# Gate and up of a transformer block's last row block from seven half products instead of eight

## The chip, the cores and the metric

The kernel runs on one core of a Trainium2 chip: TensorE (matmuls, with its own path for loading weights), VectorE, ScalarE, POOL (GpSimd) for elementwise work, and SP, whose queue issues nearly all transfers between the memories. The metric is device time in microseconds of one execution, compared by the median of several.

## The reference

One layer over x of 2048 x 1024 (float32), with D_FF = 2816:

```
a = rms_norm(h, ln_mix_pre);  proj = a @ w_in           # split among four mixers
mix = concat[S5, HGRN2, FoX, mLSTM] @ w_out             # all causal in time
h = h + rms_norm(mix, ln_mix_post)
a = rms_norm(h, ln_ffn_pre)
ff = (silu(a @ w_ffn_gate) * (a @ w_ffn_up)) @ w_ffn_down
h = h + rms_norm(ff, ln_ffn_post)
```

What concerns us here is `a @ w_ffn_gate` and `a @ w_ffn_up`, both 2048 x 1024 by 1024 x 2816.

## The kernel before

The 2048 rows are handled in four blocks of 512 (`BLK`), called first, second, third and last block here (b = 0 to 3). After the input projection of all rows, each block goes through `Attn.proj(b)` (the output projection with its norms), the mixers of the next block (`mixers(b + 1)`: mLSTM, the FoX attention and others), and the feed-forward `ffn(b)`, whose body is `run`. The mixers are written ahead of the feed-forward, so that its matmuls fill what the mixers leave of TensorE.

The order of instructions on each engine is not written out. The framework plans the program ahead of time with a simulated timeline: an instruction takes its place on its engine's queue when its inputs and its buffer are ready in that timeline, earlier lines of the program first. On the chip each queue then runs in that fixed order, and a queue whose head waits holds everything behind it.

Matmuls are made of float32 operands in two parts, high and low (a rounded value and the rest), as three matmuls: high x high, low weight x high, high weight x low. `split_load` brings weights: in the first block it loads the raw tile, ScalarE makes the high part (L87), POOL the low part (L88), and both are stored to DRAM (L92). The later blocks load the stored parts (L83). Weight tiles for gate and up lie in a ring `w_ring` of four places (tiles `wh`, `wl`), raw tiles in a ring `w_raw` of two (`wr`), tiles of x in a ring of two (`xtile`), and the weights of down in four places (`dh`, `dl`).

`Attn.proj(b)` makes, for each of four groups t of 128 rows, the second half of the output projection (L1385), the first norm and residual with a row tile `b_xt` of x (loaded at L1418, used at L1419), the second norm (L1424), and eight 128 x 128 transposes (L102) whose results are split into `b_ah` and `b_al` (ScalarE L104, VectorE L105).

In `run`, `gate_up` takes a column tile f of 128 columns of D_FF: 24 matmuls for gate and 24 for up (8 slices of the 1024 inputs, three parts), each 128 x 128 weights by 512 rows (L1468). The first pair, f = 0 and 1, is done in two halves of 256 rows each, so that it can start when t = 0 and 1 are there. Then come the gate's activation on ScalarE and VectorE (L1472 to L1478). `down` takes two tiles f at a time: 48 matmuls (L1493) in eight parts, each added into `b_acc` on VectorE (L1498). There are 22 tiles f, that is eleven pairs. The FoX attention adds its probabilities up on POOL (L900) and splits them on VectorE (L896).

## Time and profile before

| | |
|---|---|
| median of 3 runs | 2812.64 us (2810.97 to 2820.45) |
| profiled execution | 2810.77 us, its span 2809.1 us |
| TensorE busy | 2692.9 us, 96% |
| VectorE, ScalarE, POOL busy | 55%, 28%, 30% |
| DMA | 605.04 MB, mean 215 GB/s |

The span runs from the first to the last instruction of the profiled execution. A matmul's busy time includes its way through the array, in which the next one has already started; the rate at which TensorE works is the distance between two starts. "Releaser" is what ended an engine's wait.

### The profile page before, as it was taken

How to read it: one execution, taken by the hardware profiler on the slowest of the kernel's cores; microseconds unless marked ns; L12 is line 12 of the kernel's file. 1: busy time of each engine (PE TensorE's matmuls, PEld its weight loads, DVE VectorE, ACT ScalarE, POOL GpSimd, SP SyncE). 2: the span in 40 equal slices, each digit the busy share in tenths (PEclk: the TensorE clock that was granted, in tenths of full speed). 3: DMA queues.
4: the chain of work that ended last, by engine and by line, in shares of the span. 5: the costliest groups of instructions: out<-in, count | busy, mean ns of one | idle time of the engine just before them, and what ended most of it. 6: DMA issues, size and time to landing. Idle time of an engine off the chain costs nothing.

```text
span 2809.1 us, 39028 instructions
## 1 busy us (share of the span) xinstructions
PE 2692.9 (96%) x14294; PEld 2271.5 (81%) x14294; DVE 1550.5 (55%) x2522; ACT 779.0 (28%) x1502; POOL 841.8 (30%) x927
## 2 busy tenths in 40 slices
PE   6798989999999999899899999999999999999998
PEld 5787987988888778788787778888878788888886
DVE  7958456575325665876366656645666654322333
ACT  5322326322323343324221232223122331200001
POOL 7653311242216567542211234202022430100001
PEclk9999999999999999999999999999999999999999
DMA  6573695544779987686756566575656557755553
GB/s 229 201 258 114 184 300 181 169 163 161 259 205 299 317 268 267 212 306 231 273 169 215 191 199 210 174 280 195 210 181 195 193 175 246 279 198 187 194 193 136
DMA packets 323103, 605.04 MB, mean 215 GB/s; under 512 B 56160, under 2 KB 146144, under 8 KB 322656
## 3 DMA queue, kind: packets, MB, share of 16 engines
q1 hardware_dynamic: 321888, 602.48, 63.8%
q8 instruction: 113, 1.85, 0.3%
q14 instruction: 78, 0.64, 0.1%
q0 software_dynamic: 1024, 0.07, 0.0%
HBM read 428.42 MB, written 173.35 MB: 214 GB/s over the span
## 4 chain that ended last, share of the span: by engine, by line
PE 76%; DVE 8%; DMA 7%; issue 2%; SPq 2%; ACT 2%; POOL 2%; POOLq 0%; DVEq 0%; ACTq 0%
PE pf L1468 31%; PE pf L1493 15%; PE pf L288 7%; PE pf L1385 5%; PE pf L270 5%; PE ps L903 2%; DVE hQ L511 1%; PE ps L828 1%; PE ps L887 1%; PE ps L886 1%; DVE hA L525 1%; PE ps L521 1%; PE pt L102 1%; DMA b_xt<-in_x_dram 1%; DVE mcv L353 1%
## 5 line engine op out<-in xcount | busy, mean ns | idle before, releaser
L1468 PE MATMUL pf<-b_ah,wh 128*128 128x512 f32 (+1 forms) x1536 | 579.3, 378 | 4.5 <-ACT b_ah L104 4.3
L1468 PE MATMUL pf<-b_ah,wl 128*128 128x512 f32 (+1 forms) x1536 | 579.1, 378 | 0.0
L1468 PE MATMUL pf<-b_al,wh 128*128 128x512 f32 (+1 forms) x1536 | 577.5, 378 | 0.0
L1493 PE MATMUL pf<-dh,g_h 128*128 128x512 f32 x1408 | 456.8, 395 | 2.2 <-DVE b_acc L1498 1.9
L1468 PEld LDWEIGHTS pf<-b_ah,wh 128*128 128x128 f32 x1536 | 290.0, 189 | 60.4 <-ACT b_ah L104 5.3
L1468 PEld LDWEIGHTS pf<-b_ah,wl 128*128 128x128 f32 x1536 | 289.8, 189 | 54.2
L1468 PEld LDWEIGHTS pf<-b_al,wh 128*128 128x128 f32 x1536 | 288.7, 189 | 53.9
L1493 PEld LDWEIGHTS pf<-dh,g_h 128*128 128x128 f32 x1408 | 263.8, 188 | 58.8 <-DVE b_acc L1498 3.6
L1493 PE MATMUL pf<-dl,g_h 128*128 128x512 f32 x704 | 276.7, 393 | 0.0
L1498 DVE TENSOR_TENSOR b_acc<-b_acc,pf 128x512 f32<-128x512 f32 x320 | 216.3, 684 | 102.0 <-PE pf L1493 99.7
L900 POOL TENSOR_TENSOR f_accs<-f_accs,f_pe 128x512 f32<-128x512 f32 (+3 forms) x144 | 172.8, 1200 | 280.0 <-ACT f_pe L894 274.8
L88 POOL TENSOR_TENSOR wl<-wr,wh 128x1024 fp32r<-128x1024 f32 (+2 forms) x76 | 186.6, 2459 | 191.2 <-ACT wh L87 128.5
L896 DVE TENSOR_TENSOR f_pl<-f_pe,f_ph 128x512 fp32r<-128x512 f32 (+3 forms) x160 | 179.4, 1128 | 97.6 <-ACT f_ph L895 82.0
L288 PE MATMUL pf<-wl,aTh 128*128 128x256 f32 (+2 forms) x768 | 221.0, 288 | 0.0
L288 PE MATMUL pf<-wh,aTl 128*128 128x256 f32 (+2 forms) x768 | 220.4, 287 | 0.0
L288 PE MATMUL pf<-wh,aTh 128*128 128x256 f32 (+2 forms) x768 | 220.2, 287 | 0.0
L1473 DVE SCALAR_TENSOR_TENSOR g_th<-g_th,pf 128x512 f32<-128x512 f32 x88 | 60.3, 685 | 192.9 <-ACT g_th L1472 192.6
L1472 ACT ACTIVATE g_th<-pf 128x512 f32<-128x512 f32 x88 | 52.6, 598 | 403.3 <-PE pf L1468 403.2
L270 PE MATMUL pf<-aTh,wh 128*128 128x512 f32 (+1 forms) x400 | 160.3, 401 | 3.2 <-ACT aTh L104 3.2
L270 PE MATMUL pf<-aTh,wl 128*128 128x512 f32 (+1 forms) x400 | 157.9, 395 | 0.0
L1474 DVE TENSOR_TENSOR g_th<-g_th,pf 128x512 f32<-128x512 f32 x88 | 60.3, 685 | 176.1 <-PE pf L1468 175.7
L270 PE MATMUL pf<-aTl,wh 128*128 128x512 f32 (+1 forms) x400 | 156.8, 394 | 0.5 <-DVE aTl L105 0.5
(511 smaller groups left out, 4841.1 us busy)
## 6 DMA issues: line engine op xcount, KB each, us to landing
dh<-wd_0h SPq DMA_DIRECT2D x66, 256.0 KB
dl<-wd_0l SPq DMA_DIRECT2D x66, 256.0 KB
dh<-wd_1h SPq DMA_DIRECT2D x66, 256.0 KB
dl<-wd_1l SPq DMA_DIRECT2D x66, 256.0 KB
wr<-in_w_ffn_gate_dram SPq DMA_DIRECT2D x22, 512.0 KB
wr<-in_w_ffn_up_dram SPq DMA_DIRECT2D x22, 512.0 KB
dr<-in_w_ffn_down_dram SPq DMA_DIRECT2D x44, 256.0 KB
f_KB<-kb_d SPq DMA_DIRECT2D x80, 132.0 KB
```

The lines of the kernel that those rows point to most:

```text
L88: nc.gpsimd.tensor_tensor(lo, r, f32(hi), ALU.subtract)
L270: nc.tensor.matmul(l3(pt)[:, cut], lhsT=x[k][:, s], rhs=a[:, cut, k], start=(n == 0), stop=(n == 23))
L288: nc.tensor.matmul(pt[:, :w], lhsT=a[:, t, k], rhs=x[k], start=(n == 0), stop=(n == 23))
L896: nc.vector.tensor_tensor(pl[:, cs], pe[:, cs], f32(ph[:, cs]), ALU.subtract)
L900: nc.gpsimd.tensor_tensor(accs[:, cs], accs[:, cs], pe[:, cs], ALU.add)
L903: nc.tensor.matmul(o, lhsT=w, rhs=r[:, cs], start=(kt + n == 0), stop=(kt + n == NK))
L1385: nc.tensor.matmul(pt, lhsT=a[:, t, k], rhs=w, start=(first and i == 0), stop=(last and i == 2))
L1468: nc.tensor.matmul(l3(pt)[:, s], lhsT=x[:, k], rhs=a[:, s, k], start=(k == 0 and i == 0), stop=(k == KD - 1 and i == 2))
L1473: nc.vector.scalar_tensor_tensor(th, th, 1.0, pts[0], ALU.add, ALU.mult)
L1474: nc.vector.tensor_tensor(th, th, pts[1], ALU.mult)
L1493: nc.tensor.matmul(pt, lhsT=a[:, s], rhs=w[:, 0], start=(m == 0), stop=(m == 3 * len(fs) - 1))
L1498: nc.vector.tensor_tensor(acc[:, t, ns], acc[:, t, ns], pt, ALU.add)
```

## The change

In the last block alone, gate and up of a pair of column tiles are formed from seven products of halves. The rows (t = 0, 1 against t = 2, 3), the 1024 inputs (first and second 512) and the pair (f even, f odd) are halved, and the seven products, numbered 0 to 6 in the code, are those of a Strassen-like scheme (Winograd's form): sums of row halves (`T1` to `T4`) times sums of weight halves. A product is 24 matmuls of 128 x 128 weights by 256 rows, gate and up side by side in one PSUM tile; VectorE and ScalarE put the products together in a tile `C`, and `gated` does the activation from there.

Products 0, 2 and 5 use stored parts of plain weight halves. The other four use sums of weights: `Halves.make` forms them in the second block for gate and in the third for up, one step per pair: two raw tiles loaded, four POOL operations, four stores to DRAM. In the last block `Halves.load` brings such a sum into the ring's low tile, and ScalarE and POOL split it there. `Halves.put` takes the place of the eight transposes in `proj`: the same eight for t = 0 and 1 (products 0 and 2), twenty each for t = 2 and 3. There the x tile lies in `w_raw` and not in the x ring. The transposed operands lie in a tile `U`, which takes the place of the mixers' buffers.

```diff
@@ -96,7 +96,7 @@
 def transpose_parts(c, pool, tag, x, dh, dl):
     nc = c.nc
-    for h in range(0, KD, 4):
+    for h in range(0, x.shape[1] // P, 4):
         pt = pool.tile([P, 512], F32, name="pt", tag=tag)
         for j in range(4):
             nc.tensor.transpose(pt[:, j * P:(j + 1) * P], x[:, (h + j) * P:(h + j + 1) * P], c.ident)
@@ -1331,6 +1331,71 @@
     c.nc.scalar.activation(junk[:, 0:n], x, AF.Square, accum_out=out)
+class Halves:
+    def __init__(self, c):
+        self.c = c
+        self.w = [x[0].rearrange("(k p) n -> p k n", p=P) for x in (c.w_ffn_gate, c.w_ffn_up)]
+        self.pairs = c.w_ffn_gate.shape[2] // (2 * P)
+        self.sums = {(q, i): c.dram.tile([P, D], F32, name=f"ws{q}_{i}") for q in range(self.pairs) for i in (1, 3, 4, 6)}
+    def make(self, pool, q, m):
+        nc = self.c.nc
+        rs = [pool.tile([P, D], F32, name=n, tag=n) for n in ("ws_1", "ws_2")]
+        for i, r in enumerate(rs):
+            f = 2 * q + i
+            nc.sync.dma_start(r.rearrange("p (k n) -> p k n", k=KD), self.w[m][:, :, f * P:(f + 1) * P])
+        (X11, X12), (X21, X22) = ((r[:, 0:512], r[:, 512:]) for r in rs)
+        for i, s, x, y, op in ((3, X11, X11, X21, ALU.subtract), (4, X21, X21, X22, ALU.add),
+                               (1, X22, X22, X11, ALU.subtract), (6, X12, X12, X22, ALU.subtract)):
+            nc.gpsimd.tensor_tensor(s, x, y, op)
+            nc.sync.dma_start(self.sums[q, i][:, m * 512:m * 512 + 512], s)
+    def load(self, q, i):
+        c, nc = self.c, self.c.nc
+        hi, lo = (c.pw.tile([P, WRING], F32R, name=n, tag=n)[:, 0:D] for n in ("wh", "wl"))
+        if (q, i) in self.sums:
+            nc.sync.dma_start(f32(lo), self.sums[q, i])
+            nc.scalar.activation(hi, f32(lo), AF.Copy)
+            nc.gpsimd.tensor_tensor(lo, f32(lo), f32(hi), ALU.subtract)
+        else:
+            k0, f = {0: (0, 0), 2: (512, 0), 5: (512, 1)}[i]
+            for t, part in ((hi, 0), (lo, 1)):
+                for m, n in enumerate("gu"):
+                    nc.sync.dma_start(f32(t[:, m * 512:m * 512 + 512]),
+                                      c.parts[f"w{n}{2 * q + f}"][part][:, k0:k0 + 512])
+        return hi, lo
+    def operand(self, i, t):
+        u = self.U[:, 2 * i + t].rearrange("p (d k t) -> p d k t", d=2, k=4)
+        return u[:, 0], u[:, 1]
+    def put(self, t, xs, rows):
+        c, nc = self.c, self.c.nc
+        a, b = slice(0, 512), slice(512, D)
+        if t < 2:
+            new = ((0, xs[t][:, a]), (2, xs[t][:, b]))
+        else:
+            x, x1 = xs[t - 2], xs[t]
+            s1, s2 = rows(), rows()
+            T1, T2, T3, T4 = s1[:, a], s1[:, b], s2[:, a], s2[:, b]
+            nc.vector.tensor_tensor(T1, x1[:, a], x[:, a], ALU.subtract)
+            nc.vector.tensor_tensor(T2, x1[:, b], T1, ALU.subtract)
+            nc.gpsimd.tensor_tensor(T3, x1[:, b], x1[:, a], ALU.subtract)
+            nc.vector.tensor_tensor(T4, x[:, b], T2, ALU.subtract)
+            new = ((1, T2), (3, T3), (4, T1), (5, T4), (6, x1[:, b]))
+        for i, v in new:
+            transpose_parts(c, c.psS, "s", v, *self.operand(i, t % 2))
 class Attn:
@@ -1360,7 +1425,7 @@
             nc.sync.dma_start(y, c.y_d[b][t * P:(t + 1) * P])
             transpose_parts(c, c.psS, "s", y, self.ah[:, t], self.al[:, t])
-    def proj(self, b):
+    def proj(self, b, halves=None):
         c, nc = self.c, self.c.nc
         ah, al = self.ah, self.al
         wo = c.w_out[0].rearrange("(k p) n -> p k n", p=P)
@@ -1404,6 +1469,7 @@
         ws = list(weights(1))
         ws = ws
         half = c.mhalf
+        xs = []
         for t in range(4):
             pt = ptile()
             for w in ws:
@@ -1413,7 +1479,10 @@
             rs = self.ps.tile([P, 1], F32, name="b_rs")
             nc.gpsimd.tensor_scalar(rs, ss[:, t, 0:1], ss[:, t, 1:2], 1.0 / D, ALU.add, ALU.mult)
             nc.gpsimd.tensor_tensor(rs, rs, half, ALU.pow)
-            xt = self.xtile("b_xt")
+            if halves is None or t < 2:
+                xt = self.xtile("b_xt")
+            else:
+                xt = c.pwr.tile([P, WRING], F32, name="b_xt2", tag="wr")[:, 0:D]
             r0 = b * BLK + t * P
             nc.sync.dma_start(xt, c.x[0, r0:r0 + P, :])
             nc.vector.scalar_tensor_tensor(at, at, rs, xt, ALU.mult, ALU.add)
@@ -1422,7 +1491,11 @@
             square_sum(c, at, rs)
             rsqrt_mean(c, rs, rs, D)
             nc.vector.scalar_tensor_tensor(xt, at, rs, g_pre, ALU.mult, ALU.mult)
-            transpose_parts(c, c.psS, "s", xt, ah[:, t], al[:, t])
+            if halves is None:
+                transpose_parts(c, c.psS, "s", xt, ah[:, t], al[:, t])
+            else:
+                xs.append(xt)
+                halves.put(t, xs, self.row)
 def feed_forward(c, ctx, attn):
@@ -1449,7 +1522,7 @@
     def ptile():
         return c.psF.tile([P, 512], F32, name="pf", tag="f")
-    def run(b, hook):
+    def run(b, hook, step, halves):
         ah, al = attn.ah, attn.al
         acc = attn.acc()
         last = b == c.T // BLK - 1
@@ -1478,6 +1551,64 @@
                 nc.vector.scalar_tensor_tensor(lT, th, 0.5, f32(hT), ALU.mult, ALU.subtract)
                 pend.append((f, hT, lT))
+        def gate_up_halves():
+            C = attn.p.tile([P, 4, D], F32, name="g_c", tag="b_al").rearrange("p t n -> p (t n)")
+            C = C.rearrange("p (b q j m t) -> p b q j m t", b=2, q=2, j=2, m=2)
+            def product(q, i):
+                wh, wl = halves.load(q, i)
+                pt = ptile()
+                pv = pt.rearrange("p (m j t) -> p m j t", m=2, j=2)
+                for m in range(2):
+                    for k in range(4):
+                        for n, (w, d) in enumerate(((wh, 0), (wl, 0), (wh, 1))):
+                            k0 = (4 * m + k) * P
+                            nc.tensor.matmul(pv[:, m], lhsT=w[:, k0:k0 + P],
+                                             rhs=halves.U[:, 2 * i:2 * i + 2, d * 512 + k * P:d * 512 + (k + 1) * P],
+                                             start=(k == n == 0), stop=(k == 3 and n == 2))
+                return pt.rearrange("p (m t) -> p m t", m=2)
+            def add(dst, pt, x):
+                nc.vector.tensor_tensor(dst, pt, x, ALU.add)
+            def gated(f, v):
+                th, h = p2.tile([P, BLK], F32, name="g_th", tag="th"), h_tile()
+                t, h4 = (x.rearrange("p (j t) -> p j t", t=256) for x in (th, h))
+                nc.scalar.activation(t, v[:, :, 0], AF.Tanh, scale=0.5)
+                nc.vector.scalar_tensor_tensor(t, t, 1.0, v[:, :, 0], ALU.add, ALU.mult)
+                nc.vector.tensor_tensor(t, t, v[:, :, 1], ALU.mult)
+                nc.scalar.activation(h4[:, 0:2], t, AF.Copy, scale=0.5)
+                nc.vector.scalar_tensor_tensor(h4[:, 2:4], t, 0.5, f32(h4[:, 0:2]), ALU.mult, ALU.subtract)
+                pend.append((f, h[:, 0:BLK], h[:, BLK:]))
+            def head(q):
+                c1 = C[:, q % 2, 0]
+                nc.scalar.activation(c1[:, 1], product(q, 0), AF.Copy)
+                add(c1[:, 0], product(q, 2), c1[:, 1])
+            def tail(q):
+                c1, c2 = C[:, q % 2, 0], C[:, q % 2, 1]
+                add(c1[:, 1], product(q, 1), c1[:, 1])
+                add(c2[:, 0], product(q, 3), c1[:, 1])
+                pt = product(q, 4)
+                add(c1[:, 1], pt, c1[:, 1])
+                add(c2[:, 1], pt, c2[:, 0])
+                add(c1[:, 1], product(q, 6), c1[:, 1])
+                gated(2 * q, c1)
+                add(c2[:, 0], product(q, 5), c2[:, 0])
+                gated(2 * q + 1, c2)
+            for q in range(NF // 2):
+                if q == 0:
+                    head(0)
+                    head(1)
+                elif q > 1:
+                    head(q)
+                tail(q)
+                if q:
+                    down(pend[:2], q == 1)
+                    del pend[:2]
         def down(fs, first):
             def weights(n):
                 return [split_load(c, pd, attn.pdr, "d", 512, (1, 512),
@@ -1505,12 +1636,18 @@
                 part(n, t, ws[n])
         pend = []
-        gate_up((0, 1), (slice(0, 2), slice(2, 4)))
-        for f in range(2, NF):
+        if halves is not None:
+            gate_up_halves()
+        else:
+            gate_up((0, 1), (slice(0, 2), slice(2, 4)))
+        for f in range(2, NF if halves is None else 0):
+            if f % 2 == 0:
+                step(f // 2 - 1)
             gate_up((f,), (slice(0, 4),))
             if len(pend) == 3 and f < NF - 1:
                 down(pend[:2], pend[0][0] == 0)
                 pend = pend[2:]
+        step(NF // 2 - 1)
         if last:
             fin = finish(b, acc)
             next(fin)
@@ -1664,12 +1801,28 @@
     with ExitStack() as s:
         ffn = feed_forward(c, s, attn)
         c.side = "left"
+        halves = Halves(c)
+        sums = None
+        def step(b, q):
+            if 0 < b < NB - 1:
+                for m in range((b - 1) * 2 // (NB - 2), b * 2 // (NB - 2)):
+                    halves.make(sums, q, m)
         for b in range(NB):
+            last = b == NB - 1
+            if last:
+                stack.close()
+                pool = s.enter_context(tc.tile_pool(name="g_u", bufs=1, side="left", reuse_waits="tile"))
+                halves.U = pool.tile([P, 14, D], F32R, name="g_U")
             if b:
-                attn.proj(b)
+                attn.proj(b, halves if last else None)
+            if b == 1:
+                stack = ExitStack()
+                sums = stack.enter_context(tc.tile_pool(name="w_sums", bufs=1, side="left", reuse_waits="tile"))
             if b + 1 < NB:
                 mixers(b + 1)
-            ffn(b, lambda: attn.pre(b + 1) if b + 1 < NB else None)
+            ffn(b, lambda: attn.pre(b + 1) if b + 1 < NB else None, lambda q: step(b, q), halves if last else None)
```

## Rows read from the trace of the kernel before

**Rows 1.** The page: span, and each engine's busy time, share, instructions.

```profile
span 2809.1 us, 39028 instructions
...
PE 2692.9 (96%) x14294; PEld 2271.5 (81%) x14294; DVE 1550.5 (55%) x2522; ACT 779.0 (28%) x1502; POOL 841.8 (30%) x927
```

**Rows 2.** Waits of TensorE, whole run: us in total, times, longest.

```profile
PE pt L102 <- DVE b_xt L1424: 5.9, 3, 2.6
PE pf L1468 <- ACT b_ah L104: 4.3, 4, 1.4
```

**Rows 3.** Stretches: length, busy (count) of PE, PEld, DVE, ACT, POOL; clock, DMA share, GB/s.

```profile
1391.00:1864.00 473.00, 469.89 (x2372) 386.87 (x2373) 279.68 (x450) 118.67 (x239) 119.14 (x138) 1.00 0.60 200
1911.00:2379.00 468.00, 464.89 (x2251) 378.79 (x2252) 267.13 (x402) 118.47 (x231) 110.18 (x113) 1.00 0.59 197
2379.00:2427.00 48.00, 46.64 (x211) 38.03 (x211) 22.28 (x25) 12.27 (x28) 9.50 (x17) 1.00 0.81 294
2427.00:2785.00 358.00, 355.98 (x1648) 294.16 (x1648) 105.72 (x153) 30.59 (x52) 2.79 (x5) 1.00 0.56 189
...
2060.00:2300.00 240.00, 240.00 (x1086) 191.43 (x1085) 148.39 (x194) 78.87 (x154) 86.76 (x76) 1.00 0.58 189
```

**Rows 4.** Chain of waits, last block: start us, us, what.

```profile
2475.24 22.30 PE pf L1468 x96
2497.54 10.90 PE pf L1493 x48
```

**Rows 5.** Timeline of TensorE, first pair of the last block: start us, us.

```profile
2432.05 0.28 PE L1468 MATMUL pf<-b_ah,wl 128*128 128x256 f32 x1
...
2438.05 0.28 PE L1468 MATMUL pf<-b_al,wh 128*128 128x256 f32 x1
```

**Rows 6.** Timeline of TensorE, a stretch of the input projection.

```profile
298.83 0.28 PE L288 MATMUL pf<-wh,aTh 128*128 128x256 f32 x1
...
306.20 0.28 PE L288 MATMUL pf<-wh,aTl 128*128 128x256 f32 x1
```

**Rows 7.** Instructions of L1468: duration ns min/median/max, first and last start us.

```profile
L1468 PEld LDWEIGHTS pf<-b_ah,wh x1536: 186/188/333, 827.2 to 2784.1; 128*128 128x128 f32 x192
```

**Rows 8.** Timeline of the last block's projection: start us, us, engine, idle before.

```profile
2419.99 0.33 SPq L1418 DMA_DIRECT2D b_xt<-in_x_dram  x1
...
2423.74 1.28 DVE L1419 SCALAR_TENSOR_TENSOR b_acc<-b_acc,b_rs,b_xt 128x1024 f32<-128x1024 f32 x1 [2.25 <-DMA b_xt<-in_x_dram]
2424.41 1.03 PE L102 MATMUL pt<-ident,b_xt 128*128 128x128 f32 x8
2427.54 0.33 SPq L1418 DMA_DIRECT2D b_xt<-in_x_dram  x1
2428.82 0.55 POOL L1415 TENSOR_TENSOR b_rs<-b_rs,mhalf 128x1 f32<-128x1 f32 x1
2435.57 1.28 DVE L1419 SCALAR_TENSOR_TENSOR b_acc<-b_acc,b_rs,b_xt 128x1024 f32<-128x1024 f32 x1 [2.09 <-DMA b_xt<-in_x_dram]
```

**Rows 9.** Instructions of L87, L88 and L1478: duration ns min/median/max.

```profile
L87 ACT ACTIVATE wh<-wr x76: 1040/1059/1088, 11.1 to 1267.5; 128x1024 fp32r<-128x1024 f32 x72, 128x1056 fp32r<-128x1056 f32 x2, 128x1040 fp32r<-128x1040 f32 x2
L88 POOL TENSOR_TENSOR wl<-wr,wh x76: 2347/2398/2979, 13.2 to 1268.6; 128x1024 fp32r<-128x1024 f32 x72, 128x1056 fp32r<-128x1056 f32 x2, 128x1040 fp32r<-128x1040 f32 x2
L88 POOL TENSOR_TENSOR dl<-dr,dh x44: 1261/1297/2272, 851.1 to 1299.5; 128x512 fp32r<-128x512 f32 x44
L1478 DVE SCALAR_TENSOR_TENSOR g_h<-g_th,g_h x88: 654/692/4589, 842.1 to 2786.7; 128x512 fp32r<-128x512 f32 x88
```

**Rows 10.** Waits of SP's queue, 830 to 1300 us: total, times, longest.

```profile
SPq L92 <- POOL wl L88: 54.0, 32, 3.2
```

**Rows 11.** DMA of the stretch 830 to 1300 us.

```profile
DMA packets 93417, 129.40 MB, mean 275 GB/s; under 512 B 10328, under 2 KB 57080, under 8 KB 93255
```

**Rows 12.** Instructions of L896: duration ns min/median/max.

```profile
L896 DVE TENSOR_TENSOR f_pl<-f_pe,f_ph x160: 277/1172/2137, 505.8 to 2297.3; 128x512 fp32r<-128x512 f32 x112, 128x384 fp32r<-128x384 f32 x16, 128x256 fp32r<-128x256 f32 x16, 128x128 fp32r<-128x128 f32 x16
```

## The prediction

> **What bounds the kernel now.** I read the page's busy shares first, then TensorE's waits, the stretches by stage, the chain of waits of the last block, and last the single instructions. TensorE is busy 2692.9 of 2809.1 us [rows 1]. Its waits are few, and none of them is for a weight tile or for the transfer of one: the list names transposes and norms at the starts of stages [rows 2]. The feed-forward stretches of the second, third and last block run TensorE 99% busy at granted clock 1.00, which is the 2.4 GHz level, and in the attention part of the third block it has no idle time at all [rows 3]. The chain of waits of the last block is TensorE nearly throughout: ten times 22.30 us of gate and up for a pair of column tiles, 10.90 us of down between [rows 4]. VectorE, ScalarE and POOL are busy 30%, 9% and 1% of that stretch [rows 3]. So time goes when TensorE streams fewer columns there, as long as nothing new is late.
>
> **The change, part by part.** *Columns.* Before, eleven pairs of tiles make 960 matmuls of 512 columns and, in the first pair, 192 of 256. 96 of the wide ones take 22.30 us, 0.2323 each [rows 4]. The 256-wide start every 0.1132 us (53 intervals in 6.00 us [rows 5]). Gate and up are 10 x 22.30 + 192 x 0.1132 = 244.7 us. After, a pair is 7 products x 24 = 168 matmuls of 256 columns, 1848 in all. Their price is bounded from both sides: 0.1132 [rows 5], and 0.1189 in the input projection (62 intervals in 7.37 us [rows 6]). I take half of a wide one, 0.1162, which lies between: 214.7 us. That takes 30.0 us away; by the ends, 35.5 and 25.0.
>
> One doubt is the weight load: one takes 0.188 us [rows 7], more than a half-width matmul's interval. But rows 5 have one load per matmul too and still start every 0.1132, so two loads must be under way at once. The Trainium skill's page "TensorE: Matmul & The Clock Gate", section "Back-to-back issue gap", speaks against the change: it gives streams of load and matmul about 81 ns at 128 columns and 131 ns at 512. A straight line between makes an estimate of 98 ns at 256, so 1848 halves would cost 181 us against 138 for 1056 full ones, 43 us more. The trace disagrees with both ends, having 113 to 119 ns and 232 ns, nearly in proportion to columns.
>
> *Transposes.* For the rows t=2 and 3 of the last block, five half-rows each are transposed in place of two: 24 more transposes at 1.03/8 = 0.13 us [rows 8], +3.1 us. Their twelve more evictions on ScalarE and VectorE (0.6 us each) and the eight sums lie beside the four first products, 96 matmuls or 11.2 us, which need only t=0 and 1.
>
> *The norm chain of t=2 and 3.* Before, x for t=2 was issued at 2419.99 and used at 2423.74; x for t=3, whose buffer came free only after t=1's transposes, was issued at 2427.54 and used at 2435.57, though its factor was ready at 2429.37 [rows 8]. TensorE then waited 1.8 us for t=3. After, these two x tiles lie in another ring and can load early, so that wait can go. Against that stand two dependent sums more (0.7 us each) ahead of t=3's first transpose, and VectorE has about 8 us more to do in some 17 (three sums and three evictions of 0.7 for each of the two). I take 0, with ends of -2 (the wait gone) and +4 (VectorE late).
>
> *Supply of the last block.* Three products of a pair read stored high and low parts (four transfers of 256 KB each), four read one 512 KB sum that ScalarE and POOL split in the ring. With four ring places, a load starts when the product four earlier has ended, so it has three products' time, 3 x 24 x 0.1162 = 8.37 us. The first four products of a pair also have the 10.90 of down; products 4 and 6 don't. From issue to the split tile it takes 3.75 (t=2's x, also 512 KB, with its wait for a quiet engine in it) + 1.06 on ScalarE + 2.40 on POOL = 7.2 us, so nothing is late; or, with t=3's landing and the slowest split, 8.03 + 1.06 + 2.98 = 12.1 us [rows 8, 9], 3.7 us late. A late product 4 moves the rest of its pair along, so it counts once in each of eleven pairs: 0 to 41 us. The slow landing came behind a burst of weight transfers, when the stage moved 294 GB/s; the pair loop moved 189 [rows 3]. After, a pair is 7.3 MB (5.2 for the products, 2.1 for down) in 19.5 + 10.9 us, 241 GB/s, between the two and away from the burst. I take 0.2 us a pair, +2 us. Behind the splits on ScalarE and POOL nothing else of weight is queued there; behind a load on SP's queue stand down's weights, which have a whole pair of time. The product sums on VectorE, seven of 0.69 us more a pair, fit in its 70% idle.
>
> *Second and third block.* Each of 22 steps adds two loads of 512 KB, four POOL operations of 128x512 (1.30 us [rows 9]) and four stores of 256 KB: per block 57 us on POOL, which is busy 119 of 473, and 23 MB, which make 249 GB/s out of 200 [rows 3]. A store waits for its POOL operation, and on SP's queue the ring's next weight loads stand behind it. These are issued three tiles ahead, 3 x 24 x 0.2323 = 16.7 us, and need 3.75, so SP may be held some 13 us before TensorE notices. The first block's feed-forward does more of the same: it splits its raw weights on POOL, SP waited 32 times for that before a store, 3.2 us at the longest [rows 10], and its DMA moved 275 GB/s with most packets short [rows 11], yet no wait for a weight is in rows 2. I take +2 us; the ends are -6 (all of TensorE's idle time there, 3.1 + 3.1 us, won by another order) and, if each of 88 operations held TensorE for its whole length, +114, which the first block's rows put far away.
>
> The last pair's down and the tail after it stay. The sum: -30.0 + 3.1 + 0 + 2 + 2 = -22.9 us on the profiled execution's 2810.77 (span 2809.1), that is 2787.9. The median of the runs shown is 1.9 us above that execution, so I forecast 2790.
>
> **Rivals.** *The split sums come late (slower).* Place: products 4 and 6 of each pair. It decides where the chain of landing and split passes 8.37 + 24.9/11 = 10.6 us, because the other terms sum to -24.9. With the 12.1 us of the bad case the pairs lose 41 us: 2829. For it: t=3's landing; the transfers come in smaller pieces, and reads of down share the queue. Against: the loop's transfer rate is well below the burst's, and down's 10.9 us refill the ring. A mild form, 1.2 us a pair, gives 13 back: 2801.
>
> *POOL's sums hold VectorE up in the attention of the second and third block.* Place: the subtraction that splits the probabilities (L896), median 1.17 us where the same shape elsewhere on VectorE has 0.69, with 4.59 once beside POOL [rows 9, 12]. If the some 40 sums that fall into attention cost TensorE 0.7 us each, 28 are gone: 2816. It decides at 24.9/40 = 0.6 us each. Against: in rows 3 TensorE has no idle time there although L896 is already stretched. The Trainium skill's page "SBUF — State Buffer", section "Who interferes with whom", has the rule: a VectorE instruction with two SBUF inputs and a POOL instruction that reads SBUF exclude each other for their whole length. The trace agrees as far as the 4.59 goes.
>
> *The halves cost more than half.* If a weight load could not be hidden, 1848 x 0.188 = 347 us, 103 more than now, and 2922 in all; it decides at (244.7 - 7.1)/1848 = 0.1286 us per matmul. Rows 5 and 6 have every such matmul below that. The Trainium skill's rule of the issue gap, weighed above, falls on this side.
>
> **How the numbers follow.** Forecast 0.63; mild supply loss 0.14; late sums 0.10; POOL against VectorE 0.11, of which most is no change and a little slower; dear halves 0.02. The forecast's own range is 2772 to 2804. With the mild loss and part of the POOL case inside, and the far low end cut, 2777 to 2808 holds 8 in 10. No change is within 0.3%, 8.4 us, about what a measurement of this kernel can tell. Faster: 0.63 + 0.14 = 0.77. Same: 0.10 of POOL's. Slower: 0.10 + 0.02 + 0.01 = 0.13.
>
> **What the profile after would show.** Right: in the pair loop's chain of waits, pieces of 19 to 20 us for gate and up where 22.30 stood, down still 10.90, and no wait of TensorE for a split tile or a transfer; the 256-wide intervals at 0.113 to 0.119; the wait before t=3's transposes gone or under 2 us; the windows of the second and third block within 3 us of 473 and 468. Wrong: a TensorE wait on POOL or a ring transfer ahead of product 4 in each pair; idle TensorE in the second or third block's attention with VectorE's L896 or SP's stores named; intervals near 0.188; or a granted clock of 0.5 after a stall in the last block's projection.

## The result and the profile after

The changed kernel takes 2834.88 us (median of six runs, 2826.95 to 2840.76), the kernel before 2811.8 beside it. The ratio is 1.0085, with an interval of 1.0068 to 1.0102: it is slower, by some 24 us. The forecast was 2790, faster; the prediction was wrong.

The page of the changed kernel's profiled execution, to be held against [rows 1]: TensorE is as busy as before, though it streams fewer columns, and POOL is busy 231 us more.

```profile
span 2839.1 us, 41291 instructions
...
PE 2691.8 (95%) x15014; PEld 2302.7 (81%) x15014; DVE 1640.8 (58%) x2611; ACT 833.7 (29%) x1563; POOL 1072.5 (38%) x1061
```

The stretches of the changed kernel that answer to [rows 3] (columns as there): the second block from its first gate and up to the third block's projection, the third block likewise, the last block's projection, its pair loop.

```profile
1399.00:1906.00 507.00, 482.45 (x2373) 394.43 (x2374) 278.72 (x452) 119.99 (x241) 226.06 (x218) 0.98 0.82 269
1953.00:2423.00 470.00, 466.37 (x2251) 380.01 (x2252) 267.80 (x402) 118.51 (x232) 110.17 (x113) 1.00 0.60 196
2423.00:2470.00 47.00, 46.75 (x212) 38.11 (x210) 23.13 (x25) 12.62 (x28) 9.55 (x18) 1.00 0.80 277
2470.00:2804.00 334.00, 326.64 (x2317) 304.21 (x2316) 184.98 (x230) 84.66 (x111) 113.20 (x50) 1.00 0.72 238
```

The second block went from 473 to 507 us, the third from 468 to 470. POOL shows why the two differ so: 226 us against 119 in the second block, 110 against 110 in the third. All 22 steps ran in the second block. The raw loads by line, changed kernel (duration ns min/median/max, first and last start us):

```profile
L1352 SPq DMA_DIRECT2D ws<-in_w_ffn_gate_dram x22: 383/386/2116, 1347.3 to 1559.7; - x22
L1352 SPq DMA_DIRECT2D ws<-in_w_ffn_up_dram x22: 383/384/534, 1575.9 to 1768.1; - x22
```

The code gives the up steps to the third block, and the description of the change says so too, but they depend only on inputs and on their own two buffers, and in the trace they follow the gate steps without a pause.

By the starts of the projections the profiled executions compare so, in us: up to the second block's projection 1332.4 before and 1336.1 after (+3.7); second block 531.6 and 569.8 (+38.2); third 515.2 and 517.4 (+2.2); last block to the end 429.8 and 415.8 (-14.0). Together, but for rounding, +30.0, the difference of the spans (of one execution each; the one after is the longest of its six). So two things want explaining: a loss of 38 us in the second block where 2 for both blocks were forecast, and a gain of 14 in the last block where 25 was.

**The second block.** In the first of the stretches above TensorE's idle time is 507 - 482.45 = 24.6 us, before 3.1. Its busy time is 12.6 longer for the same matmuls, at a granted clock of 0.98 instead of 1.00. So of the 34 us that this stretch grew by, 21.4 are waits and 12.6 a lower clock. What it waited for, 1395 to 1900 us (total, times, longest):

```profile
PE ps L828 <- DMA f_KB<-kb_d: 8.3, 2, 5.3
PE pf L1624 <- DVE b_acc L1629: 5.1, 1, 5.1
PE pt L102 <- DVE b_xt L1493: 3.4, 2, 3.1
PE ps L886 <- DMA f_KA<-ka_d: 2.2, 1, 2.2
```

Both of the longest waits can be followed back. The first goes through SP's queue; its timeline (start us, us, what), and POOL's instruction that it waited for:

```profile
1602.90 0.75 SPq L83 DMA_DIRECT2D wh<-wg11h  x1
1610.29 4.61 SPq L1357 DMA_DIRECT2D ws<-ws  x4
...
1619.35 0.38 SPq L783 DMA_DIRECT2D f_KB<-kb_d  x1
```

```profile
1608.86 1.41 POOL L1356 TENSOR_TENSOR ws<-ws,ws 128x512 f32<-128x512 f32 x1 [8.79 <-DMA ws<-in_w_ffn_up_dram]
```

A store of a sum (L1357) held SP from 1603.7, when the issue before it was done, to 1610.3, when POOL had the sum; POOL had waited 8.8 us for the raw tile. With the three stores after it, SP was held to 1614.9. The attention's load of keys (f_KB) came behind, was issued at 1619.4 and landed when TensorE had waited 5.3 us for it, at 1625.9. The 6.5 us from issue to landing are part of that too; the trace alone doesn't say how long they would have been without the other transfers. The second wait goes through POOL's queue; POOL and VectorE, in two timelines:

```profile
1759.74 2.98 POOL L1356 TENSOR_TENSOR ws<-ws,ws 128x512 f32<-128x512 f32 x2
1772.31 1.29 POOL L1356 TENSOR_TENSOR ws<-ws,ws 128x512 f32<-128x512 f32 x1 [9.59 <-DMA ws<-in_w_ffn_up_dram]
1775.05 0.19 POOL L67 TENSOR_SCALAR f_ms<-f_ms 128x4 f32<-128x4 f32 x1
1776.54 1.02 POOL L68 TENSOR_TENSOR f_ms<-f_ms,mhalf 128x4 f32<-128x4 f32 x1
```

```profile
1766.12 0.42 DVE L861 TENSOR_REDUCE f_ms<-f_sq 128x4 f32<-128x256 f32 x1 [0.54 <-ACT f_sq L859]
1777.59 1.48 DVE L863 TENSOR_TENSOR f_o<-f_o,f_ms 128x256 f32<-128x256 f32 x1 [7.65 <-POOL f_ms L68]
1778.99 0.67 DVE L1629 TENSOR_TENSOR b_acc<-b_acc,pf 128x512 f32<-128x512 f32 x1
```

The factor of a norm was ready for POOL at 1766.5. Ahead of it in POOL's queue a sum waited 9.6 us for its raw tile. VectorE then waited 7.7 for the factor, with the evictions of down queued behind, and TensorE 5.1 for those. A wait of one queue thus passes through two more. The clock adds to it: in the stretches that begin right after these two waits the granted clock is 0.70 and 0.71, that is partly the lower level of 1.2 GHz.

```profile
1626.00:1636.00 10.00, 10.00 (x31) 7.87 (x32) 5.46 (x6) 2.50 (x5) 9.83 (x9) 0.70 0.81 247
...
1779.70:1790.00 10.30, 10.28 (x33) 8.20 (x34) 5.93 (x10) 1.76 (x6) 6.29 (x10) 0.71 1.06 392
```

**The last block.** Its chain of waits has, for [rows 4], gate and up of a pair at 20.07 us and down at 11.08 in the best pairs:

```profile
2690.54 20.07 PE pf L1566 x168
2710.61 11.08 PE pf L1624 x48
```

From start to start of TensorE's matmuls, whole block: gate and up 247.2 us before, 225.5 after (-21.7); down 120.1 and 127.0 (+6.9); transposes 5.3 and 7.4 (+2.1); the rest, mostly the tail, -1.3. That is the -14.0.

### The profile page after: what moved, and what is told of

Same layout as the page of the kernel before. It is cut to its first block, busy times and chain, and to the rows that moved or that the text cites. A ratio compares the mean times of both kernels' runs of the same rounds, so it can differ in the third digit from the quotient of the medians.

```text
span 2839.1 us, 41291 instructions
## 1 busy us (share of the span) xinstructions
PE 2691.8 (95%) x15014; PEld 2302.7 (81%) x15014; DVE 1640.8 (58%) x2611; ACT 833.7 (29%) x1563; POOL 1072.5 (38%) x1061
## 3 DMA queue, kind: packets, MB, share of 16 engines
q0 software_dynamic: 1024, 0.07, 0.0%
## 4 chain that ended last, share of the span: by engine, by line
PE 69%; DMA 10%; DVE 10%; POOL 3%; issue 3%; ACT 2%; SPq 1%; POOLq 0%; DVEq 0%; ACTq 0%
PE pf L1541 20%; PE pf L1624 13%; PE pf L288 7%; PE pf L1566 6%; PE pf L270 5%; PE pf L1450 5%; PE ps L903 2%; DMA wl<-ws 2%; DVE hQ L511 1%; PE ps L828 1%; PE ps L886 1%; PE ps L887 1%; DVE hA L525 1%; POOL ws L1356 1%; PE ps L521 1%
## 5 line engine op out<-in xcount | busy, mean ns | idle before, releaser
L1624 PE MATMUL pf<-dh,g_h 128*128 128x512 f32 x1408 | 463.1, 398 | 11.2 <-DVE b_acc L1629 10.0
L1541 PE MATMUL pf<-b_ah,wh 128*128 128x512 f32 (+1 forms) x1152 | 438.6, 381 | 3.6 <-ACT b_ah L104 1.8
L1541 PE MATMUL pf<-b_ah,wl 128*128 128x512 f32 (+1 forms) x1152 | 438.6, 381 | 0.0
L1541 PE MATMUL pf<-b_al,wh 128*128 128x512 f32 (+1 forms) x1152 | 436.7, 380 | 0.0
L88 POOL TENSOR_TENSOR wl<-wr,wh 128x1024 fp32r<-128x1024 f32 (+2 forms) x76 | 187.0, 2463 | 197.2 <-ACT wh L87 142.1
L1541 PEld LDWEIGHTS pf<-b_ah,wh 128*128 128x128 f32 x1152 | 220.0, 191 | 45.4 <-ACT b_ah L104 2.3
L1629 DVE TENSOR_TENSOR b_acc<-b_acc,pf 128x512 f32<-128x512 f32 x320 | 213.8, 682 | 73.8 <-PE pf L1624 72.4
L1541 PEld LDWEIGHTS pf<-b_ah,wl 128*128 128x128 f32 x1152 | 219.7, 191 | 40.9
L896 DVE TENSOR_TENSOR f_pl<-f_pe,f_ph 128x512 fp32r<-128x512 f32 (+3 forms) x160 | 166.4, 1046 | 121.0 <-ACT f_ph L895 108.1
L1566 PE MATMUL pf<-g_U,wh 128*128 128x256 f32 x1232 | 223.0, 283 | 1.4 <-ACT wh L1365 0.9
L1566 PEld LDWEIGHTS pf<-g_U,wh 128*128 128x128 f32 x1232 | 190.6, 190 | 4.0 <-DVE b_acc L1629 1.3
L1366 POOL TENSOR_TENSOR wl<-wl,wh 128x1024 fp32r<-128x1024 f32 x44 | 108.9, 2485 | 210.0 <-ACT wh L1365 206.9
L1566 PE MATMUL pf<-g_U,wl 128*128 128x256 f32 x616 | 172.4, 282 | 2.3 <-POOL wl L1366 2.3
L894 ACT ACTIVATE f_pe<-ps 128x512 f32<-128x512 f32 (+3 forms) x160 | 85.3, 533 | 274.0 <-PE ps L887 105.3
```

The costliest lines, as they stand in the source:

```text
L88: nc.gpsimd.tensor_tensor(lo, r, f32(hi), ALU.subtract)
L894: nc.scalar.activation(pe[:, cs], pt[:, cs], AF.Exp)
L896: nc.vector.tensor_tensor(pl[:, cs], pe[:, cs], f32(ph[:, cs]), ALU.subtract)
L1366: nc.gpsimd.tensor_tensor(lo, f32(lo), f32(hi), ALU.subtract)
L1541: nc.tensor.matmul(l3(pt)[:, s], lhsT=x[:, k], rhs=a[:, s, k], start=(k == 0 and i == 0), stop=(k == KD - 1 and i == 2))
L1566: nc.tensor.matmul(pv[:, m], lhsT=w[:, k0:k0 + P], rhs=halves.U[:, 2 * i:2 * i + 2, d * 512 + k * P:d * 512 + (k + 1) * P], start=(k == n ...
```

## The experiments

Each result is the median, then the ratio to the kernel before with its 95% interval. The length of a block goes from the start of its projection to the start of the next one, in the one profiled execution of each kernel. Such lengths move by some 5 us without a cause in the block's own code (the last block, same code, is 415.8 us in the changed kernel, 420.4 in e3_no_pool, 420.5 in e4_paced), so smaller differences are no evidence.

**The last block's gain without the sums (e1_no_sums).** In the changed kernel's main program and in `load`:

```
-                    halves.make(sums, q, m)
+                    pass
...
-            nc.sync.dma_start(f32(lo), self.sums[q, i])
+            nc.sync.dma_start(f32(lo), c.parts[f"w{'gu'[i % 2]}{2 * q}"][0])
```

> The changed kernel without the forming of the sums: no raw weight loads, POOL sums or stores in the second and third block. The last block does all its seven products, but where it loads a formed sum it loads a stored high part of 512 KB instead (so the products have other numbers). Theory A (the loss lies in forming the sums in the second block, +38 us there in the traces, and the last block gains 14): the second block falls back to 532 us, the whole to 2811.8 - 14 = 2798 (2793 to 2802). Rival B (the second block is longer for another reason, such as other buffers or another order of the work that the change brings): the second block stays at 560 to 570 and the whole at 2830 or more.

2795.54 us, ratio 0.9947 (0.9931 to 0.9962). The second block is back at 529.7. Theory A holds, B falls.

**The sums without the gain (e2_sums_only).**

```
-                attn.proj(b, halves if last else None)
+                attn.proj(b)
...
-            ffn(..., lambda q: step(b, q), halves if last else None)
+            ffn(..., lambda q: step(b, q), None)
```

> The changed kernel with only the forming of the sums: they are loaded, formed and stored, and nobody reads them; the last block computes gate and up with eight products as before. Theory A: the second block costs +38 and the last block gains nothing, 2811.8 + 38 to 44 = 2850 to 2856. Rival B (forming is free, the loss comes from the last block's new buffers): 2812. A middle value would say that the two parts of the change disturb each other.

2854.93 us, 1.0155 (1.0131 to 1.0178), second block 578.3. The two parts simply add: -15 and +43 give +28, and the change as a whole has +24 (19 to 29).

**The transfers without POOL's sums (e3_no_pool).**

```
         for i, s, x, y, op in ...:
-            nc.gpsimd.tensor_tensor(s, x, y, op)
             nc.sync.dma_start(self.sums[q, i][...], s)
```

> The changed kernel without the four POOL subtractions and additions of each step: the raw tiles are loaded and their halves stored unsummed, so all transfers stay (46 MB) and the last block's sums have other numbers. Theory P (POOL's queue and its 1.3 to 2.5 us operations hold the attention's own POOL work and VectorE): the second block is back within 5 us of 532, the whole near 2800. Theory S (the stores and loads hold SP's queue ahead of the attention's and the weights' loads): stores still wait for the raw loads' landing, though not for POOL (39 and 19 us of SP's waits stay, 71 go), so about half the loss stays, 2815 to 2825. Theory D (DMA engines 86 to 98% busy delay all transfers): bytes are the same, 2828 or more.

2815.1 us, 1.0022 (1.0008 to 1.0035); second block 547.7. That is what theory S gave. Of 40 us over the kernel without sums (529.7), 22 go with POOL's sums, by their place in POOL's queue and by the stores that wait for them on SP's; 18 stay with the transfers, by what stands behind them on SP's queue or by the load on the DMA engines. This run does not part the two ways of either share. D as the only cause falls, since this second block moves 278 GB/s at a DMA share of 0.84, no less than the changed kernel's; P falls with the 18. One place of the 18 is seen at the start of the block, in SP's timeline of this kernel (L1356 is the store here, L1661 the output step of the block before, loading its residual rows):

```profile
1346.91 1.87 SPq L1352 DMA_DIRECT2D ws<-in_w_ffn_gate_dram  x2
...
1355.01 0.42 SPq L1661 DMA_DIRECT2D g_h<-h_d  x1
1355.90 4.16 SPq L1356 DMA_DIRECT2D ws<-ws  x4
...
1362.29 0.32 SPq L1661 DMA_DIRECT2D g_h<-h_d  x1
```

Two raw loads stand ahead of the first g_h, the four stores of a step ahead of the second; the first was issued at 1355.0, in the kernel before at 1346.9. VectorE, which needs g_h before it can evict the projection, stood idle 19.8 us there (11.2 before), and TensorE waited 16.4 at the projection (8.6 before, 4.1 in the kernel without sums).

**Eleven steps in each block (e4_paced).** The weight load keeps its instruction (`c.loaded = nc.sync.dma_start(...)`, L83), and what a step issues on SP is put behind it:

```
-                for m in range((b - 1) * 2 // (NB - 2), b * 2 // (NB - 2)):
-                    halves.make(sums, q, m)
+                with tc.issue_after(c.loaded.ins):
+                    halves.make(sums, q, b - 1)
```

> The changed kernel with the eleven gate steps in the second block and the eleven up steps in the third, each tied to its place: its loads and stores stand on SP's queue behind a weight load of the feed-forward, so that they can't move ahead into the attention of the block. Same transfers, POOL operations and stores in all. Theory C (concentration: 22 steps in one block fill its DMA to 86 to 98% and SP's and POOL's queues; eleven in a block don't): second and third block together lose at most 10 us, the whole is 2800 to 2808. Rival I (each step costs about 1.7 us of TensorE wherever it stands): 22 x 1.7 = 38 stays, 2830 to 2840.

2808.65 us, 1.0000 (0.9988 to 1.0012). Second block 539.2, third 519.2: together 12 us over the kernel without sums instead of 40. A price per step, rival I, would have kept the 38. This is the work as the prediction assumed it, eleven steps in a block and one to a pair; it cost 12 us, or 15 by the ratios (1.0000 against 0.9947), where 2 were forecast.

**The price of a half by itself (e5_halves_before).** The kernel before, with

```
-            gate_up((f,), (slice(0, 4),))
+            gate_up((f,), (slice(0, 2), slice(2, 4)) if last else (slice(0, 4),))
```

> The kernel before, with gate and up of the last block done for 256 rows and then for the other 256 (in before only its first pair is): 960 matmuls of 512 columns become 1920 of 256, with the same weights, sums and transfers. It prices a half by itself. Theory N (a half costs 0.1132, as the first pair's intervals): 960 x (2 x 0.1132 - 0.2323) = -5.7 us. Theory H (in a long run of halves one costs 0.119 to 0.120, as measured in the products of the changed kernel): 960 x (2 x 0.1195 - 0.2323) = +6.4 us. So 2804 or 2816 beside 2810; anything above 2830 would speak for a weight load that isn't hidden.

2806.75 us, 1.0000 (0.9989 to 1.0012). A half is not dear in a long run of halves: the time lies between theory N's -5.7 us and theory H's +6.4, and gate and up of the last block take 243.9 us from start to start, 247.2 before. The chain of waits has 192 of them in 21.97 us, 0.1144 each:

```profile
2638.76 21.97 PE pf L1468 x192
```

Within a pair some 48 take 0.118 and the other 144 take 0.1133. So the 0.119 of the products belongs to the products. The issue gap of the Trainium skill (page "TensorE: Matmul & The Clock Gate", section "Back-to-back issue gap"), by whose figures the prediction estimated that halves cost more than half, is not seen here: 2 x 0.1144 is 0.2288, below the 0.2323 of a full one, and the measurement decides.

**The split of the sums on VectorE (e6_split_vector).** Paced steps as above, and in `load`

```
-            nc.gpsimd.tensor_tensor(lo, f32(lo), f32(hi), ALU.subtract)
+            nc.vector.tensor_tensor(lo, f32(lo), f32(hi), ALU.subtract)
```

> The kernel with paced steps (e4_paced), and in the last block the low part of each split sum formed on VectorE in place of POOL. Theory X (POOL's 2.4 us splits hold VectorE's sums that read two SBUF tiles, 0.69 us become 2.3 to 2.5, and through them the eviction of the down products: 7 us of waits for b_acc): the waits go, VectorE gets 44 x 1.3 us more in 364, the time is 2801 to 2804. Rival Q (VectorE's queue is the limit; splits that wait there for a landing hold the evictions longer): 2808 or more.

2803.47 us, 0.9984 (0.9972 to 0.9997), the last block's feed-forward (from the first product to the end of down's last matmul) 354.2 against 362.9 in e4_paced. That is 9 us in the profiled executions, but 4.5 by the ratios (1.0000 to 0.9984), whose intervals overlap. TensorE's waits for the eviction of down (b_acc, L1629) in the last block fall from 5.9 us to 0.3. VectorE's instructions of the last block by line (count | busy us, mean ns | idle before), first of the changed kernel:

```profile
L1579 DVE TENSOR_TENSOR g_th<-g_th,g_c 128x512 f32<-128x512 f32 x22 | 33.6, 1529 | 0.4
L1578 DVE SCALAR_TENSOR_TENSOR g_th<-g_th,g_c 128x512 f32<-128x512 f32 x22 | 32.9, 1494 | 14.0 <-ACT g_th L1577 14.0
```

and of this one:

```profile
L1578 DVE SCALAR_TENSOR_TENSOR g_th<-g_th,g_c 128x512 f32<-128x512 f32 x22 | 15.1, 688 | 7.6 <-ACT g_th L1577 7.6
L1579 DVE TENSOR_TENSOR g_th<-g_th,g_c 128x512 f32<-128x512 f32 x22 | 15.1, 686 | 0.3
```

The gating reads SBUF twice now (gate and up lie in g_c, before they lay in PSUM). Beside a POOL split it took up to 2.8 us, as in the changed kernel here, in VectorE's and POOL's timelines:

```profile
2651.49 2.48 DVE L1578 SCALAR_TENSOR_TENSOR g_th<-g_th,g_c 128x512 f32<-128x512 f32 x1 [1.42 <-ACT g_th L1577]
2653.90 0.68 DVE L1629 TENSOR_TENSOR b_acc<-b_acc,pf 128x512 f32<-128x512 f32 x1
2654.49 2.29 DVE L1579 TENSOR_TENSOR g_th<-g_th,g_c 128x512 f32<-128x512 f32 x1
```

```profile
2651.01 5.22 POOL L1366 TENSOR_TENSOR wl<-wl,wh 128x1024 fp32r<-128x1024 f32 x2 [10.86 <-ACT wh L1365]
```

The eviction between them, which reads PSUM and SBUF, kept its 0.68, but had to queue. This is the rule of the Trainium skill's page "SBUF — State Buffer", section "Who interferes with whom": a VectorE instruction with two SBUF inputs contends with a POOL instruction that reads SBUF, one with a single SBUF input does not. The trace agrees with it in this place. Theory X holds.

**No split at all (e8_no_split).** Paced steps kept, and in `load`

```
-            nc.gpsimd.tensor_tensor(lo, f32(lo), f32(hi), ALU.subtract)
```

> The kernel with paced steps (e4_paced), with the low part of each split sum left out of the last block (the tile is used as loaded, so the products have other numbers); the matmuls, transfers and VectorE's work stay. Theory X: VectorE's sums of two SBUF tiles fall from 2.3 to 2.5 back to 0.69 us and the waits for b_acc go: 2800 to 2803. Rival V (the b_acc waits come from VectorE's own added work, seven product sums a pair): sums stay long or waits stay, 2807 to 2810.

2800.31 us, 0.9969 (0.9958 to 0.9981), 9 us below e4_paced by the ratios and clear of their intervals; gating at 0.69 us, feed-forward 350.6, and no wait of TensorE for b_acc in the last block. Down takes 121.2 us from start to start, with the split on VectorE 124.9, with it on POOL (e4_paced) 130.9. VectorE's added product sums are not what held the evictions; rival V falls.

**Steps in the middle of the blocks (e7_mid_vector).** The split on VectorE, and

```
+        when = {2: (0,), 3: (1, 2), 4: (3,), 5: (4, 5), 6: (6,), 7: (7, 8), 8: (9,), 9: (10,)}
...
+                for n in when.get(q, ()):
                     with tc.issue_after(c.loaded.ins):
-                        halves.make(sums, q, b - 1)
+                        halves.make(sums, n, b - 1)
```

> The kernel of e6_split_vector, with the eleven steps of each block kept away from both ends of its feed-forward (none in the first pairs nor in the last ones, some slots with two steps). Theory T (what paced steps still cost, about 12 us over the kernel without sums, are the waits at the starts of the stages, where norms, last block's output and projections wait for loads behind the steps' transfers on SP's queue): second and third block fall to within 3 us of 530 and 517, and the whole is some 8 us below e6_split_vector, 2793 to 2797. Rival I (each step costs wherever it stands): the same as e6_split_vector within 2 us.

2793.48 us, 0.9953 (0.9935 to 0.9970): faster than the kernel before, and than the changed one. Second block 534.5, third 516.6; theory T. It has some 13 us (8 to 18) of the 23 forecast. In the profiled execution the last block gains 18.8 us (429.8 to 411.0) and the two others lose 4.1.

**All steps in the middle of the second block (e11_one_block).** As the last, but

```
-            if 0 < b < NB - 1:
+            if b == 1:
                 for n in when.get(q, ()):
+                    for m in range(2):
...
-                        halves.make(sums, n, b - 1)
+                            halves.make(sums, n, m)
```

> The kernel of e7_mid_vector, with all 22 steps in the second block again, but kept to the middle of its feed-forward as there (two or four at a place). It tells how many from where. Theory C (the number of transfers and POOL operations in one block is what costs; 22 steps in one block fill the DMA engines above 86%): the second block stays 20 us or more above 530, the whole 2810 or more. Theory T (the place decides: only steps that reach into the starts of stages hold something up): second block within 10 us of 535, the whole 2793 to 2800.

2835.11 us, 1.0106 (1.0090 to 1.0123), second block 572.1. Theory C: place alone doesn't save it. The windows of the second block, 22 steps and eleven, steps in the middle in both:

```profile
1392.00:1900.00 508.00, 479.33 (x2330) 389.88 (x2329) 279.38 (x447) 117.85 (x236) 237.38 (x223) 0.97 0.82 271
```

```profile
1392.00:1863.00 471.00, 465.27 (x2334) 381.83 (x2333) 273.56 (x446) 118.47 (x236) 179.35 (x179) 1.00 0.75 246
```

TensorE's idle time is 28.7 us in the one and 5.7 in the other.

**No steps, else as with steps in the middle (e13_mid_none).** With steps in the middle, but

```
-                        halves.make(sums, n, b - 1)
+                        pass
```

and stored high parts loaded in place of the sums, as in e1_no_sums.

> The kernel of e7_mid_vector without the forming of the sums; the last block loads stored high parts of the same size in their place (other numbers). The difference to e7_mid_vector is all that 22 steps still cost when kept to the middle of two blocks. Theory T (place and number were all of the cost): within 4 us of e7_mid_vector, 2789 to 2793. Rival I (a price for each step stays): 8 or more below it, 2785 or less.

2794.75 us, 0.9942 (0.9923 to 0.9960). Theory T: no cost of the 22 steps spread over the middle of two blocks shows in the time. The two ratios are 3 us apart, and their intervals leave some 7 us either way. In the profiled executions the second block is 8 us longer with the steps (534.5 against 526.5), the last block 6 shorter.

**Where the products' 0.119 is from.** Four edits of the kernel with steps in the middle. First, another tile as the moving operand (e9_rhs_ah):

```
-  rhs=halves.U[:, 2 * i:2 * i + 2, d * 512 + k * P:d * 512 + (k + 1) * P],
+  rhs=ah[:, 2 * d:2 * d + 2, k],
```

> The kernel of e7_mid_vector, with the products' moving operand read from the tile that the projection used (b_ah, two row tiles at 4 KB from each other) in place of g_U; the products have other numbers. In e5_halves_before a half costs 0.1145 on the mean (0.1133 for most, 0.118 for the first 48 of a pair), in the products 0.1194. Theory U (where the operand lies in SBUF makes the difference): the products' intervals fall to 0.113 to 0.115, the last block by some 9 us. Rival O (the order of a product does it: 24 matmuls each into two halves of one PSUM bank, evicted once per product): the intervals stay at 0.119 to 0.120.

2787.11 us, 0.9933 (0.9906 to 0.9959), of two runs; most intervals are 0.113 or 0.114: theory U. But this operand holds other values too. Then the two pieces of an operand side by side (e10_side_by_side):

```
-                halves.U = pool.tile([P, 14, D], F32R, name="g_U")
+                halves.U = pool.tile([P, 7, 2 * D], F32R, name="g_U")
...
+  rhs=halves.U[:, i, (4 * d + k) * 256:(4 * d + k) * 256 + 256],
```

> The kernel of e7_mid_vector, with the two row tiles of an operand laid side by side in g_U, so that a product's moving operand is 256 columns in a row instead of two times 128 at 4 KB from each other. It computes the same. Theory L (the step between the two pieces costs about 5 ns a matmul; the down products, whose 512 columns lie in a row, start every 0.2265, twice 0.1133): 1848 x (0.1194 - 0.1133) = 11 us less, 2782 to 2785. Rival O (order or operand place): intervals stay at 0.119, 2793.

2800.18 us, 0.9969 (0.9956 to 0.9983): intervals at 0.120, L falls. Then g_U in two tiles (e14_two_tiles), and g_U at the other end of SBUF (e12_right):

```
-                halves.U = pool.tile([P, 14, D], F32R, name="g_U")
+                halves.U = [pool.tile([P, 14, 512], F32R, name=n) for n in ("g_U", "g_V")]
...
```

```
-  tc.tile_pool(name="g_u", bufs=1, side="left", reuse_waits="tile")
+  tc.tile_pool(name="g_u", bufs=1, side="right", reuse_waits="tile")
```

> The kernel of e7_mid_vector, with the high and the low parts of the operands in two tiles of half the row length (2 KB from row tile to row tile instead of 4), as b_ah and b_al were two tiles. It computes the same. Theory A: another address pattern, so another interval, in either direction, 0.113 to 0.120. Rival W: 0.119 to 0.120 as before.

> The kernel of e7_mid_vector, with g_U at the other end of SBUF (beside b_ah and not beside the weight rings). It computes the same. Theory A (the address of the moving operand sets the interval): the products' 0.1194 changes, towards 0.113 to 0.115 if the neighbourhood of b_ah is what counts, the last block is some 8 us shorter, 2785. Rival W (what was written into the operand, or how it is cut, and not its place): intervals stay at 0.119 to 0.120, 2793.

Two tiles: 2797.98 us, 0.9957 (0.9939 to 0.9974), intervals mostly 0.120. The other end: 2795.63 us, 0.9946 (0.9931 to 0.9961). The chain of waits has a product loop of 168 matmuls, with steps in the middle, with the other tile, and with g_U at the other end:

```profile
2580.73 20.04 PE pf L1566 x168
```

```profile
2551.36 19.25 PE pf L1566 x168
```

```profile
2650.89 19.26 PE pf L1566 x168
```

That is 0.1193, 0.1146 and 0.1146 a matmul, at a granted clock of 1.00 in all three. What is written in g_U at the other end is the same, so its place sets the interval: theory A, and the order of a product, rival O, falls. Which property of the place does it stays open. In time the move brought nothing that can be told apart: products 224.6 to 218.3 us from start to start, but down 124.5 to 128.0; why stays open.

## Why the prediction was wrong

In the profiled executions -22.9 us was forecast and +30.0 measured. Of the 52.9 between, 38.3 lie in the second and third block, 6.9 in down, 6.3 in gate and up with their supply, 3.7 ahead of the second block, and -2.3 in the transposes and the tail.

- *Second and third block, +2 us:* this step failed. It counted eleven steps in each block, "23 MB, which make 249 GB/s out of 200". The trace has 22 in one, at 269 GB/s, and +38 us. What was not looked at is what binds a step to its block: nothing did. The size was off for the work as assumed, too: eleven steps a block, one to a pair, cost 12 us (e4_paced), and only away from both ends of the block's feed-forward no cost shows. The upper end of the term, +114, would have covered the 38, but the only chance given to a loss there, 0.11, was for one mechanism, POOL against VectorE.
- *"SP may be held some 13 us before TensorE notices":* nearly true for the ring's weights (one wait of 1.6 us), and wrong for what else stands on SP's queue. Attention's keys, the residual rows of the output and x come with much less lead. The first block ([rows 10, 11]) was no evidence that such work is free. It was asked only for waits for weights, and there are none; but its stretch as a whole, in the columns of [rows 3], has TensorE idle 14.6 us at a granted clock of 0.97, where the second block's has 3.1 at 1.00. How much of that comes from the splitting no run shows.

```profile
830.00:1300.00 470.00, 455.40 (x2317) 377.63 (x2316) 309.26 (x451) 164.23 (x286) 262.73 (x202) 0.97 0.83 275
```

- POOL's queue was costed by busy time (57 us of idle 354), not by what stands behind a sum that waits for its raw tile. The norm factors and the attention's sums do, and 22 of the 40 us went with POOL's sums.
- *POOL against VectorE in attention (rival):* the mechanism is real, and the place was wrong. L896 was not longer in the second block (median 0.70 us after, 1.27 before). It struck in the last block, where the change itself makes two-SBUF instructions of the gating and puts 44 splits on POOL: without the split 9 us came back (e8_no_split).
- *Columns, -30.0:* 225.5 after holds 5.3 of stalls, so 220.2 for 1848, 0.1192 each where 0.1162 was taken, and above the upper end of 0.1189. The row of the first pair, 0.1132, was right for its own operand, and e5_halves_before is near it; an interval does not carry over to an operand in another place.
- *Supply, +2 us (0 to 41):* stalls of 5.3 us in all and no pair waits at products 4 and 6 regularly. The first rival falls: of TensorE's waits in the pair loop only 2.3 us name POOL's split and 0.9 ScalarE's.
- *Down unchanged:* it lost 6.9 us (120.1 to 127.0), through the evictions behind the stretched gating; without the split (e8_no_split) it is 121.2.
- *Transposes and norm chain:* +2.1 for +3.1, and the wait ahead of t=3's transposes is gone, as its lower end had it. Dear halves, the third rival, fell.

## What to carry to other kernels

Work that depends on nothing but inputs has no place in time of its own: before costing it against a stage's slack, find what keeps it in that stage, and bind it if nothing does. Cost an instruction that waits on an in-order queue by everything behind it that has a short lead, through to the engines that wait for those. When operands move from PSUM to SBUF, look at who else reads SBUF beside them on POOL.

## What the runs showed of the hardware

The same product loop on TensorE starts a 256-wide matmul every 0.1193 us or every 0.1146, by the place of its moving operand in SBUF, at a granted clock of 1.00 either way; the operand's layout (two pieces or one, one tile or two) made no difference at the first place. And VectorE's gating, with both inputs in SBUF, took 1.49 to 1.53 us on the mean beside POOL's splits and 0.69 without them.
